# One more pair of up-projection tiles by half-size products, with the last gate's first half summed during the out-projection

## The chip, the cores and the metric

The kernel runs on one core of a Trainium2 chip. Times are microseconds (us) of device time, the median of several runs; beside it stands one profiled execution, whose trace gives the time of each instruction.

The engines are named as in the profile: PE is TensorE (PEld its weight loads), DVE is VectorE, ACT is ScalarE, POOL is GpSimd, SP is SyncE, which here only issues transfers. ACT and POOL issue some transfers too.

## The reference

One decoder layer on 512 tokens of width 1024, all in float32. Sub-layer 1 is a normalised, modulated input projection, two groups of heads (a gated recurrence of 4 heads, and sparse attention), and an output projection. Sub-layer 2, which the change touches most, is a gated MLP of width 2816 with a causal depthwise convolution over 3 tokens:

```python
mod = cs @ w_ada[l] + b_ada[l]
sh1, sc1, gt1, sh2, sc2, gt2 = [m[:, None, :] for m in jnp.split(mod, 6, axis=-1)]
...
x = x + gt1 * mix
h2 = rmsnorm(x, norm2_g[l]) * (1.0 + sc2) + sh2
u = causal_dwconv(h2 @ w_up[l], conv_w[l], conv_b[l])
a, v = jnp.split(u, 2, axis=-1)
x = x + gt2 * ((jax.nn.silu(a) * v) @ w_down[l])
```

Here `cs` is silu of the conditioning vector `c`. The last gate, `gt2`, is a row of 1024 numbers, the product of `cs` with 1024 columns of `w_ada`.

## The kernel before

**Numbers.** A float32 matrix is split into a high and a low part (`split`: ScalarE copies to the rounded type, VectorE subtracts), and a product is three matmuls: high by high, high by low, low by high (`mm3`, lines 156 to 158). Some low parts are formed without VectorE: ScalarE writes the negated rounded value, and a transfer from GpSimd's queue adds the source to it (`added`, lines 260 and 1695).

**Out-projection** (L1577 on). The outputs of the recurrence are normalised per row tile of 128 tokens (`hg_mix`: matmuls, square on ScalarE, sum on VectorE, the reciprocal square root `rstd`, which is one VectorE operation and one on GpSimd, then the scaling `on`), transposed (`hg_flip`) and split. Then eight blocks of the product (`out_mm`, four row tiles by two halves) are added to the residual `x1` (`out_sum`). The loop of L1948 does the second halves; for each row tile it sums squares (`out_norm`: again a root on GpSimd), scales to `hx`, transposes (`h2_flip`) and modulates and splits for the MLP.

**Up-projection.** There are 22 tiles of 128 hidden columns, each with two halves (`a` and `v`), so 44 steps numbered `st`; two tiles make a pair `j`, of four steps. A step in plain form is 8 blocks of the inner dimension by `mm3`: 24 matmuls on 512 tokens. A unit (pairs `NB` = 2 to `NU` = 8, so seven of them) computes the even tile of its pair as a 2 x 2 block product (halves of the inner dimension by halves of the tokens) in seven products instead of eight, at 4 x 3 matmuls on 256 tokens each: 84 half-width matmuls; the odd tile stays plain, 48 full-width matmuls. The first two pairs are plain (the prologue), and so are the last two (steps 36 to 43).

**What sets the order.** Every engine works through its instructions in the order of the program; that order is written out by hand, in strings of tokens: `PRO` for the prologue, `UNIT` for each unit (a prime means: of the next pair), `PLAIN` for the last steps (a leading A: the next weight's low part by an accumulating transfer; the digit: how many steps of the gate). `P1` to `P7` are products, `p` is the convolution, `n`, `s`, `f` form sums and splits of weights, `x` takes one entry from a list of splits of finished values, `g` advances the gate. So an instruction that waits holds up what stands behind it on its engine.

**The gate** (`ada_last`). `gt2` is built in two halves of 512 columns. Each is eight transfers of 128 x 512 weights and eight multiply-adds on VectorE, then a split and two matmuls with a matrix of ones, and a copy back. All transfers are in SyncE's queue. The first half goes through one buffer (the second half of `gt2` itself), one transfer and multiply-add per `g`: three in the prologue and one in each unit. The second half goes through buffers of the general pool during the plain steps.

**Memory.** Most long-lived blocks lie in 33 granules of 4 KB per partition. The finished values of the MLP are kept as `gP`, `gQ` and others for the down-projection, which is a half-size scheme again, in three phases. Where granules are short, `gQ` of the pairs in `AWAY` is written to memory (`park`, from ScalarE's queue) and read back during the first phase (`load_away`); its products stand in the second phase.

Of the kernel before, what the change touches and what calls it, by code (L numbers as in the profile page):

```python
# [20 lines left out]
P = 128  # L21
# [19 lines left out]
NB = 2  # L41
NU = 8
AWAY = (0, 1)
CUT = {"B": 6, "C": 7}
ADD = (1, 1)
PLAIN = "2 A1 1 1 A2 1 1 1"
PRO = ("t t g x M1 M2 t t t t F3 M3 F4 t A5 q0 M4 q1 q2 F6 q3 M5 M6 A7 x q4 g x q5 x t x n1' ns' f2' nc' n5' q6 na' g s4' m0' x x M7 m1' x f6' f7' x x x x f4'")
UNIT = ("P1 S P5 w n1' ns' x f3 B0 P6 P2 B1 V x f2' nc' n5' h1 x p-1 f4' P7 x m0' P3 h0' W p2 g p0 na' C0 P4 x x x C1 s4' p1 x m1' x f6' x x x f7'")
# [63 lines left out]
def hybrid_layer_kernel(ctx: ExitStack, tc: tile.TileContext, d: dict, out: bass.AP, dbg=None):  # L112
# [1164 lines left out]

    def hg_mix(i):
        ps = PS("hgo")
        for h in range(4):  # L1280
            AD, QP, S = As[h // 2]
            j = h % 2
            pe.matmul(ps[:, h * P:(h + 1) * P], AD[:, j, i], HV[j][:, i, h // 2 * P:h // 2 * P + P], start=True,
                      stop=(i == 0))
            if i:
                pe.matmul(ps[:, h * P:(h + 1) * P], QP[:, j, i * P:(i + 1) * P], S[:, j, i - 1], start=False, stop=True)
        sq = TMP([P, 512], tag="sqh")
        sc.activation(sq, ps, AF.Square)
        s = SM([P, 8], "hss")
        ve.tensor_reduce(s[:, 0:4], sq.rearrange("p (h e) -> p h e", h=4), AX.X, ALU.add)  # L1290
        r = SM([P, 8], "hrs")
        rstd(r[:, 0:4], s[:, 0:4], 1.0 / P, 4.0 * EPS)
        on = TMP([P, 4, P], tag="on")
        ve.tensor_tensor(on, ps.rearrange("p (h e) -> p h e", h=4),
                         r[:, 0:4].unsqueeze(2).to_broadcast([P, 4, P]), ALU.mult)
        ons[i] = on

    def hg_flip(i):
        on = ons.pop(i)
# [5 lines left out]
        for pr in range(2):  # L1305
            ve.scalar_tensor_tensor(t[:, 2 * pr:2 * pr + 2], ps[:, pr * 256:pr * 256 + 256]
                                    .rearrange("p (h t) -> p h t", h=2), hgg,
                                    HGT[pr][:, :, i * P:(i + 1) * P], ALU.mult, ALU.mult)
        split(m[:, 0], m[:, 1], t)
        mixH[i] = m  # L1310
# [88 lines left out]
    def ada_last(s, res):  # L1399
        for q in range(2):  # L1400
            acc = res[:, q * 512:(q + 1) * 512]
            c0 = s * D + q * 512
            gp.memset(acc, 0.0)
            sp.dma_start(acc[0:1], d["b_ada"][:, c0:c0 + 512])
            for k in range(KT if q else 0):
                raw = TMP([P, 512], tag="ada2r")
                sp.dma_start(raw, ada_view[:, k, c0:c0 + 512])
                if k:
                    yield
                    ve.scalar_tensor_tensor(acc, last, cs[:, k - 1:k], acc, ALU.mult, ALU.add)  # L1410
                last = raw
            for k in range(0 if q else KT):
                last = res[:, 512:]
                if k:
                    ve.scalar_tensor_tensor(acc, last, cs[:, k - 1:k], acc, ALU.mult, ALU.add)
                sp.dma_start(last, ada_view[:, k, c0:c0 + 512])
                if k < KT - 1:
                    yield
            yield
            ve.scalar_tensor_tensor(acc, last, cs[:, k:k + 1], acc, ALU.mult, ALU.add)  # L1420
            hi = TMP([P, 512], F32R, tag="rhi")
            lo = TMP([P, 512], F32R, tag="rlo")
            split(hi, lo, acc)
            yield
            ps = PS()
            pe.matmul(ps, onesr, hi, start=True, stop=False)
            pe.matmul(ps, onesr, lo, start=False, stop=True)
            sc.copy(acc, ps)
            yield


# [145 lines left out]
    for i in range(NT):  # L1577
        x1.append(G([D], s="x1"))
        sp.dma_start(x1[i], x_view[:, i])
    next(gate1)  # L1580
    hg_mix(0)
    next(gate1)
    hg_mix(1)
    out_mm(0, 0, KN)
    cols_sum(acol)
    hg_flip(0)
    hg_mix(2)
    hg_mix(3)
    out_mm(1, 0, KN)
# [4 lines left out]
    hg_flip(1)  # L1594
    hg_flip(2)
    out_mm(3, 0, KN)
# [148 lines left out]
    def do_(j, tok):  # L1745
# [30 lines left out]
        elif tok == "x":  # L1776
            step(1)
        elif tok == "g":
            next(ada2, None)
        elif tok == "t":  # L1780
# [64 lines left out]
    def park(j, st22, st34):  # L1845
        if j in AWAY:
            sc.dma_start(pk26[:, AWAY.index(j)], f32(gQ.pop(j)))
        sc.dma_start(pk22[:, j], f32(st22))
        sc.dma_start(pk34[:, j], f32(st34))
# [93 lines left out]

    gt2 = wp.tile([P, D], F32, tag="xin", name="gt2", bufs=1)
    ada2 = ada_last(5, gt2)
    lo_half, hi_half, full = slice(0, 256), slice(256, 512), slice(0, 512)
    nst = 2 * NFF
    for i in range(NT):  # L1948
# [6 lines left out]
        out_sum(i, 1)  # L1955
        sc.dma_start(x1d[:, i], x1[i])
        out_norm(i)
        if i:
            h2_scale(i - 1, 0)
            h2_scale(i - 1, 1)  # L1960
# [12 lines left out]
    for tok in PRO.split():  # L1973
# [7 lines left out]
        elif tok[0] == "q":  # L1981
            up_post(int(tok[1]))
        elif tok[0] in "txg":
            do_(1, tok)
        else:
            do(NB - 1, tok)
# [6 lines left out]
    for st in range(first, nst):  # L1993
# [7 lines left out]
        for _ in range(int(PLAIN.split()[st - first][-1])):  # L2001
            next(ada2, None)

    look()
    up_post(nst - 2, False)
# [102 lines left out]
```

## Time and profile before

| | |
|---|---|
| median of 3 runs | 674.73 us (674.6 to 674.8) |
| the profiled execution | 674.35 us, its span 672.6 us |
| granted TensorE clock | 1.0 |
| busy share of the span | PE 99%, PEld 84%, DVE 86%, ACT 58%, POOL 9% |
| out-projection, first matmul to last | 273.7 to 326 us |
| up-projection | 326.9 to 563.8 us (first unit's products from 372.3) |
| down-projection | from 564.2 us |

A row of the timeline reads: start in us, duration in us, engine, line, operation, out<-in, shape, count; in brackets the time that the engine stood idle just before, and what ended that. Matmuls are pipelined, so a matmul's duration is longer than the distance to the next one; the distance between starts is what counts. In a row of windows, each engine has its busy time and its number of instructions in that stretch.

### The profile page before, as it was taken

The numbers are of one execution on the slowest core, as the hardware profiler recorded it, in microseconds if no ns is written. First come the engines' busy times: TensorE is split into PE (matmuls) and PEld (weight loads), VectorE is DVE, ScalarE is ACT, GpSimd is POOL, SyncE is SP. The second block draws the span as 40 slices with busy tenths as digits, with TensorE's granted clock in tenths as the row PEclk, the third lists the DMA queues.
The fourth block names the chain that finished last, engine by engine and source line by source line (L and its number), as shares of the span: only waits on it lengthen the run. The fifth ranks groups of instructions, "written<-read, shape, count | busy, mean of one in ns | idle before, by whom it ended". The sixth has DMA issues, their size and how long they took to land.

```text
span 672.6 us, 10869 instructions
## 1 busy us (share of the span) xinstructions
PE 664.9 (99%) x3999; PEld 565.1 (84%) x3999; DVE 577.8 (86%) x1155; ACT 392.6 (58%) x757; POOL 60.0 (9%) x80
## 2 busy tenths in 40 slices
PE   8999999999999999999999999999999999999998
PEld 4678898788898889888998888989888888888886
DVE  5688988999998997687878988998898789988787
ACT  5564446666677688335665766667675455553431
POOL 1006144200000000200000011010110000000000
PEclk9999999999999999999999999999999999999999
DMA  9998444388042132435436677986779773979932
GB/s 279 287 322 269 145 157 138 106 288 254 11 147 95 33 107 99 172 96 161 140 95 172 179 196 198 242 218 175 187 181 277 217 234 124 393 259 398 388 112 94
DMA packets 110473, 128.52 MB, mean 191 GB/s; under 512 B 7067, under 2 KB 84691, under 8 KB 110421
## 3 DMA queue, kind: packets, MB, share of 16 engines
q1 hardware_dynamic: 103541, 106.89, 51.1%
q0 software_dynamic: 2448, 8.91, 6.9%
q10 hardware_dynamic: 4432, 12.04, 4.7%
q8 instruction: 31, 0.51, 0.3%
q14 instruction: 21, 0.17, 0.1%
HBM read 105.01 MB, written 13.90 MB: 177 GB/s over the span
## 4 chain that ended last, share of the span: by engine, by line
PE 92%; SPq 3%; DMA 2%; DVE 1%; issue 0%; ACTq 0%; ACT 0%
PE u L156 11%; PE u L158 11%; PE u L157 11%; PE dn L157 5%; PE dn L156 5%; PE dn L158 5%; PE pT L156 3%; PE pT L158 3%; PE pT L157 3%; PE F L1059 3%; PE oT L1087 3%; PE oh L158 2%; PE oh L156 2%; PE oh L157 2%; SPq L317 2%; PE lev L1188 2%
## 5 line engine op out<-in xcount | busy, mean ns | idle before, releaser
L156 PE MATMUL u<-h2h,whi 128*128 128x512 f32 (+1 forms) x208 | 78.0, 375 | 0.0
L157 PE MATMUL u<-h2l,whi 128*128 128x512 f32 (+1 forms) x208 | 77.8, 374 | 0.0
L158 PE MATMUL u<-h2h,wlo 128*128 128x512 f32 (+1 forms) x208 | 77.6, 373 | 0.0
L153 DVE TENSOR_TENSOR wlo<-raw,whi 128x1024 fp32r<-128x1024 f32 (+1 forms) x38 | 44.5, 1170 | 6.7 <-ACT whi L152 6.5
L152 ACT CAST whi<-raw 128x1024 fp32r<-128x1024 f32 (+1 forms) x38 | 38.3, 1008 | 18.8 <-PE u L157 7.3
L158 PEld LDWEIGHTS u<-h2h,wlo 128*128 128x128 f32 x208 | 39.2, 188 | 7.5 <-DVE wlo L153 0.4
L156 PEld LDWEIGHTS u<-h2h,whi 128*128 128x128 f32 x208 | 39.3, 189 | 6.0
L157 PEld LDWEIGHTS u<-h2l,whi 128*128 128x128 f32 x208 | 39.3, 189 | 5.8
L1027 ACT ACTIVATE pt<-pt,mx 128x128 f32<-128x128 f32 (+3 forms) x64 | 35.9, 562 | 11.8 <-DVE mx L1011 10.7
L1634 DVE SCALAR_TENSOR_TENSOR y<-u,cv,y 128x511 f32<-128x511 f32 x44 | 32.8, 745 | 11.4 <-ACT y L1633 11.4
L156 PE MATMUL pT<-hT,whi 128*128 128x512 f32 x96 | 39.2, 408 | 0.0
L1638 ACT ACTIVATE y<-y 128x512 f32<-128x512 f32 x21 | 13.3, 633 | 42.0 <-DVE y L1635 42.0
L158 PE MATMUL pT<-hT,wlo 128*128 128x512 f32 x96 | 37.7, 393 | 0.0
L157 PE MATMUL pT<-hT,whi 128*128 128x512 f32 x96 | 37.6, 391 | 0.0
L1011 DVE CUSTOM_DVE_ANT_0 pt<-S,cmask 128x128 f32<-128x128 f32 (+3 forms) x64 | 29.7, 484 | 6.5 <-PE S L1006 6.3
L1066 ACT COPY pT<-F 128x512 f32<-128x512 f32 (+2 forms) x52 | 25.9, 503 | 14.4 <-PE F L1059 11.2
L1635 DVE SCALAR_TENSOR_TENSOR y<-u,cv,y 128x510 f32<-128x510 f32 x44 | 32.9, 749 | 1.6
L1633 ACT ACTIVATE y<-u,cv 128x512 f32<-128x512 f32 x44 | 33.8, 771 | 0.0
L393 POOL TENSOR_TENSOR hrs<-hrs,mhalf 128x4 f32<-128x4 f32 (+2 forms) x16 | 20.0, 1259 | 136.4 <-DVE hrs L392 136.3
L157 PE MATMUL u<-h2l,w 128*128 128x256 f32 (+1 forms) x84 | 28.0, 333 | 0.0
L156 PE MATMUL u<-h2h,w 128*128 128x256 f32 (+1 forms) x84 | 28.0, 333 | 0.0
L158 PE MATMUL u<-h2h,w 128*128 128x256 f32 (+1 forms) x84 | 28.0, 333 | 0.0
(456 smaller groups left out, 2079.2 us busy)
## 6 DMA issues: line engine op xcount, KB each, us to landing
raw<-in_w_up SPq DMA_DIRECT2D x44, 512.0 KB, 5.6
aw<-in_w_ada SPq DMA_DIRECT2D x24, 512.0 KB, 3.6
raw<-in_w_down SPq DMA_DIRECT2D x10, 1024.0 KB
ada<-in_w_ada SPq DMA_DIRECT2D x32, 256.0 KB, 5.8
wlo<-raw POOLq DMA_DIRECT2D x15, 512.0 KB, 4.6
raw<-in_w_in SPq DMA_DIRECT2D x7, 1024.0 KB, 6.1
rawd<-in_w_down SPq DMA_DIRECT2D x12, 512.0 KB, 10.3
pk<-st ACTq DMA_DIRECT2D x11, 512.0 KB, 4.0
```

What stands on the lines that cost most here:

```text
L152: sc.copy(hi, src)
L153: (eng or ve).tensor_tensor(lo, src, f32(hi), ALU.subtract)
L156: pe.matmul(o, ah, bh, start=start, stop=False, skip_group_check=True)
L157: pe.matmul(o, ah, bl, start=False, stop=False, skip_group_check=True)
L158: pe.matmul(o, al, bh, start=False, stop=stop, skip_group_check=True)
L1011: ve.tensor_tensor_reduce(pt[:, sl], ps[:, sl], cmask[:, 512 - W:512], -1.0, 1e30, ALU.add, ALU.min, mx[:, e:e + 1])
L1027: sc.activation(pt[:, sl], pt[:, sl], AF.Exp, bias=mx[:, e:e + 1], scale=-1.0, accum_out=su[:, h % 2, e:e + 1])
L1059: pe.transpose(ps[:, j * P:(j + 1) * P], src[:, j * P:(j + 1) * P], ident)
L1066: sc.copy(pT, ps[:, 0:n * P])
L1633: sc.activation(y, u, AF.Identity, bias=cv[:, 132 + c:133 + c], scale=cv[:, 88 + c:89 + c])
L1634: ve.scalar_tensor_tensor(y[:, 1:], u[:, :T - 1], cv[:, 44 + c:45 + c], y[:, 1:], ALU.mult, ALU.add)
L1635: ve.scalar_tensor_tensor(y[:, 2:], u[:, :T - 2], cv[:, c:c + 1], y[:, 2:], ALU.mult, ALU.add)
```

## The change

- `NU` is 9: one more pair (steps 36 to 39) becomes a unit, and four plain steps are left.
- `AWAY` has pairs 0 to 3 instead of 0 and 1, and `park` stores them from GpSimd's queue.
- `ada_last` is made ready ahead of the out-projection, and split into finer steps: multiply-add, transfer, copy to the high part, subtraction, matmuls, copy back. Its first half has its transfers in GpSimd's queue and is advanced inside the out-projection: between the root and the scaling of `hg_mix` 1 and 3, between copy and subtraction of `hg_flip` 2, and ahead of and behind `out_norm` of each row tile. Its end (last multiply-add, split, matmuls, copy) stands in the prologue (`G`, one step each). The second half has its transfers in SyncE's queue into a part of the constants' tile and is advanced by `g` (two steps) in the units.

```diff
-NU = 8
-AWAY = (0, 1)
+NU = 9
+AWAY = (0, 1, 2, 3)
-PLAIN = "2 A1 1 1 A2 1 1 1"
-PRO = ("t t g x M1 M2 t t t t F3 M3 F4 t A5 q0 M4 q1 q2 F6 q3 M5 M6 A7 x q4 g x q5 x t x n1' ns' f2' nc' n5' q6 na' g s4' m0' x x M7 m1' x f6' f7' x x x x f4'")
+PLAIN = "1 A0 0 A0"
+PRO = ("t t x M1 M2 t t t t F3 M3 F4 t A5 G q0 G M4 q1 q2 F6 q3 M5 G M6 A7 x q4 x q5 G x t x n1' ns' f2' nc' n5' q6 na' s4' m0' x x M7 m1' g x f6' f7' x x x x f4'")
...
     def ada_last(s, res):
         for q in range(2):
             acc = res[:, q * 512:(q + 1) * 512]
+            last = cb[:, C_LMASK:C_LMASK + 512] if q else res[:, 512:]
             c0 = s * D + q * 512
             gp.memset(acc, 0.0)
-            sp.dma_start(acc[0:1], d["b_ada"][:, c0:c0 + 512])
-            for k in range(KT if q else 0):
-                raw = TMP([P, 512], tag="ada2r")
-                sp.dma_start(raw, ada_view[:, k, c0:c0 + 512])
-                if k:
-                    yield
-                    ve.scalar_tensor_tensor(acc, last, cs[:, k - 1:k], acc, ALU.mult, ALU.add)
-                last = raw
-            for k in range(0 if q else KT):
-                last = res[:, 512:]
+            gp.dma_start(acc[0:1], d["b_ada"][:, c0:c0 + 512])
+            for k in range(KT):
                 if k:
                     ve.scalar_tensor_tensor(acc, last, cs[:, k - 1:k], acc, ALU.mult, ALU.add)
-                sp.dma_start(last, ada_view[:, k, c0:c0 + 512])
-                if k < KT - 1:
-                    yield
-            yield
+                yield
+                (sp if q else gp).dma_start(last, ada_view[:, k, c0:c0 + 512])
+                yield
             ve.scalar_tensor_tensor(acc, last, cs[:, k:k + 1], acc, ALU.mult, ALU.add)
             hi = TMP([P, 512], F32R, tag="rhi")
             lo = TMP([P, 512], F32R, tag="rlo")
-            split(hi, lo, acc)
+            sc.copy(hi, acc)
+            yield
+            ve.tensor_tensor(lo, acc, f32(hi), ALU.subtract)
             yield
             ps = PS()
             pe.matmul(ps, onesr, hi, start=True, stop=False)
             pe.matmul(ps, onesr, lo, start=False, stop=True)
+            yield
             sc.copy(acc, ps)
             yield
+
+    def gate_step(n=2):
+        for _ in range(n):
+            next(ada2, None)
...
+    gt2 = wp.tile([P, D], F32, tag="xin", name="gt2", bufs=1)
+    ada2 = ada_last(5, gt2)
+    gate_step()
     next(gate1)
     hg_mix(0)
     next(gate1)
-    hg_mix(1)
+    hg_mix(1, partial(gate_step, 1))
+    gate_step(1)
...
-    hg_mix(3)
+    hg_mix(3, partial(gate_step, 1))
+    gate_step(1)
...
-    hg_flip(2)
+    hg_flip(2, partial(gate_step, 1))
+    gate_step(1)
...
     def park(j, st22, st34):
         if j in AWAY:
-            sc.dma_start(pk26[:, AWAY.index(j)], f32(gQ.pop(j)))
+            gp.dma_start(pk26[:, AWAY.index(j)], f32(gQ.pop(j)))
...
         sc.dma_start(x1d[:, i], x1[i])
+        gate_step(1)
         out_norm(i)
+        gate_step(1)
```

GpSimd's instructions in the out-projection, before (`hrs` and `rs` are the roots of the two normalisations, `hgA` belongs to the recurrence ahead of it, `gt` is `gt2`, `wlo` a low part of an up-projection weight):

```order
L1151 MEMSET hgA_1916 128x1024
L393 TENSOR_TENSOR hrs_3331<-hrs_3331,mhalf 128x4
L393 TENSOR_TENSOR hrs_3353<-hrs_3353,mhalf 128x4
L393 TENSOR_TENSOR hrs_3400<-hrs_3400,mhalf 128x4
L393 TENSOR_TENSOR hrs_3418<-hrs_3418,mhalf 128x4
L393 TENSOR_TENSOR rs_3307<-rs_3307,mhalf 128x1 x4
L1403 MEMSET gt_3611 128x512
L260 DMA wlo_4101<-raw_3690 128x1024
```

And the same place now:

```order
L1407 MEMSET gt_3318 128x512
L1408 DMA gt_3318<-in_b_ada 1x16x32
L1413 DMA gt_3318<-in_w_ada 128x512
L393 TENSOR_TENSOR hrs_3335<-hrs_3335,mhalf 128x4
L393 TENSOR_TENSOR hrs_3357<-hrs_3357,mhalf 128x4
L1413 DMA gt_3318<-in_w_ada 128x512
L393 TENSOR_TENSOR hrs_3406<-hrs_3406,mhalf 128x4
L393 TENSOR_TENSOR hrs_3424<-hrs_3424,mhalf 128x4
L1413 DMA gt_3318<-in_w_ada 128x512 x2
L393 TENSOR_TENSOR rs_3307<-rs_3307,mhalf 128x1
L1413 DMA gt_3318<-in_w_ada 128x512
L393 TENSOR_TENSOR rs_3307<-rs_3307,mhalf 128x1
```

The eight transfers of the gate's first half stand among the roots; the last four follow the four roots of `out_norm` one by one.

VectorE in the last row tile of the out-projection's loop, now (`x` is the residual, `ss` the sum of squares, `hx` the scaled row):

```order
L1511 TENSOR_TENSOR tmp_3858<-oh_3816,gt_90_713 128x512
L1512 TENSOR_TENSOR x_656_3316<-x_656_3316,tmp_3858 128x512
L1411 SCALAR_TENSOR_TENSOR gt_3318<-gt_3318,cs 128x512
L1517 TENSOR_TENSOR ss_3306<-ss_3306 128x1
L392 TENSOR_SCALAR rs_3307<-ss_3306 128x1
L1547 TENSOR_SCALAR hB_3874<-ps_3846,a_711,sh_712 128x128 x4
L1524 TENSOR_SCALAR hx_3879<-x_656_3316,rs_3307 128x512 x2
```

Before, the same rows stood there without the third, the gate's multiply-add.

VectorE at the end of the prologue, before (`raw` is a weight as loaded, `w` and `wlo` low parts of weights, `e` a sum of two quarters of a weight):

```order
L153 TENSOR_TENSOR w_809_4242<-e_4245,w_809_4242 128x512
L1634 SCALAR_TENSOR_TENSOR y_4253<-u_4186,cv,y_4253 128x511
L1635 SCALAR_TENSOR_TENSOR y_4253<-u_4186,cv,y_4253 128x510
L1685 TENSOR_TENSOR raw_4089<-e_4245,raw_4089 128x512
L1415 SCALAR_TENSOR_TENSOR gt_3611<-gt_3611,cs 128x512
L1685 TENSOR_TENSOR raw_4089<-raw_4089 128x512
L153 TENSOR_TENSOR wlo_4266<-raw_4147,whi_4265 128x1024
```

And now:

```order
L153 TENSOR_TENSOR w_812_4263<-e_4266,w_812_4263 128x512
L1642 SCALAR_TENSOR_TENSOR y_4274<-u_4208,cv,y_4274 128x511
L1643 SCALAR_TENSOR_TENSOR y_4274<-u_4208,cv,y_4274 128x510
L1693 TENSOR_TENSOR raw_4103<-e_4266,raw_4103 128x512
L1693 TENSOR_TENSOR raw_4103<-raw_4103 128x512
L153 TENSOR_TENSOR wlo_4285<-raw_4166,whi_4284 128x1024
```

The gate's multiply-add between the two subtractions on the weight is gone from this place.

More of the change, by code (lines that the diff above doesn't have):

```diff
@@ L1276, in hybrid_layer_kernel, with hg_mix @@
     mixH = [None] * NT
-    def hg_mix(i):
+    def hg_mix(i, between=lambda: None):
         ps = PS("hgo")
@@ L1292, in hg_mix @@
         rstd(r[:, 0:4], s[:, 0:4], 1.0 / P, 4.0 * EPS)
+        between()
         on = TMP([P, 4, P], tag="on")
@@ L1296, in hg_mix, with hg_flip @@
         ons[i] = on
-    def hg_flip(i):
+    def hg_flip(i, between=lambda: None):
         on = ons.pop(i)
@@ L1308, in hg_flip @@
                                     HGT[pr][:, :, i * P:(i + 1) * P], ALU.mult, ALU.mult)
-        split(m[:, 0], m[:, 1], t)
+        sc.copy(m[:, 0], t)
+        between()
+        ve.tensor_tensor(m[:, 1], t, f32(m[:, 0]), ALU.subtract)
         mixH[i] = m
@@ L1777, in do_ @@
             step(1)
-        elif tok == "g":
-            next(ada2, None)
+        elif tok in ("g", "G"):
+            gate_step(2 if tok == "g" else 1)
         elif tok == "t":
@@ L1942, in dn_out @@
         sp.dma_start(out_view[:, i, cols], t)
-    gt2 = wp.tile([P, D], F32, tag="xin", name="gt2", bufs=1)
-    ada2 = ada_last(5, gt2)
     lo_half, hi_half, full = slice(0, 256), slice(256, 512), slice(0, 512)
@@ L1982, in hybrid_layer_kernel @@
             up_post(int(tok[1]))
-        elif tok[0] in "txg":
+        elif tok[0] in "txgG":
             do_(1, tok)
@@ L2001, in hybrid_layer_kernel @@
         for _ in range(int(PLAIN.split()[st - first][-1])):
-            next(ada2, None)
+            gate_step()
+    assert next(ada2, 0) == 0
     look()
```

## The prediction

> **What bounds the kernel now.** I read the page first (busy shares, then the chain of waits).
>
> ```profile
> span 672.6 us, 10869 instructions
> PE 664.9 (99%) x3999; PEld 565.1 (84%) x3999; DVE 577.8 (86%) x1155; ACT 392.6 (58%) x757; POOL 60.0 (9%) x80
> PE 92%; SPq 3%; DMA 2%; DVE 1%; issue 0%; ACTq 0%; ACT 0%
> ```
>
> TensorE is 92% of the chain that ends last; what other engines hold there lies mostly at the start, before its work begins. But a busy share of 99% is modelled, so I checked starts: second view, the stages; third, the timeline of TensorE.
>
> ```profile
> core 0: us, PE busy (x) PEld busy (x) DVE busy (x) ACT busy (x) POOL busy (x), PEclk, DMA share, GB/s
> 395.00:416.00 21.00, 21.00 (x134) 19.05 (x133) 18.63 (x34) 13.74 (x25) 1.73 (x2) 1.00 0.85 225
> 526.00:562.00 36.00, 36.00 (x161) 29.80 (x160) 29.20 (x44) 17.80 (x28) 1.75 (x2) 1.00 0.67 213
> ```
>
> The first stretch is one unit (a pair of tiles by half-size products and its two neighbours), the second lies in the plain tiles.
>
> ```profile
> 395.04 0.28 PE L156 MATMUL ux<-hS,w 128*128 128x256 f32 x1
> 395.16 0.28 PE L157 MATMUL ux<-hS,w 128*128 128x256 f32 x1
> ...
> 500.18 0.28 PE L156 MATMUL ux<-hS,w 128*128 128x256 f32 x1
> ...
> 526.13 0.39 PE L158 MATMUL u<-h2h,wlo 128*128 128x512 f32 x1
> ...
> 561.94 0.39 PE L157 MATMUL u<-h2l,whi 128*128 128x512 f32 x1
> ```
>
> From the first product into "ux" of one unit to that of five units later: 105.14 us, so 21.03 us a unit. Half-width matmuls start 0.12 us apart. In the plain stretch, 161 matmuls touch the window; two had begun before it, so 159 start between 526.13 and 561.94: 35.81/158 = 0.2266 us apart. A unit is 84 half-width and 48 full-width matmuls: 84 x 0.12 + 48 x 0.2266 = 20.96, and 21.03 was measured. So TensorE stands still for hardly 0.07 us a unit, and not at all in the plain tiles. The granted clock is 1.00 in both. Whoever wants to gain here must take matmul columns away, or one of the few real waits; whoever delays another engine pays only beyond that engine's slack.
>
> **The extra pair.** Four plain stages (two tiles, both halves of the MLP) become a unit. Before: 4 x 24 matmuls x 0.2266 = 21.75 us. After: 21.03. That takes away 0.72 us, once. The saving is one eighth of the columns of two tiles (3072 of 24576), shrunk because a half-width matmul costs 0.120 where half of a full one is 0.113: 84 x 0.0067 = 0.56 us is lost that way.
>
> The Trainium skill (TensorE: Matmul & The Clock Gate, "Wait — 56ns, not 53.3ns?") puts warm starts at N/2.4 GHz plus about 2.5 ns. That would be 0.2158 and 0.1092 us, and a saving of 48 x 0.2158 - 84 x 0.1092 = 1.18 us, an estimate from that page. The trace differs at both widths (0.2266, 0.120), so the sum goes by 0.72.
>
> Can VectorE feed one more unit? It is busy 18.63 of 21 us in one, and five in a row cost no time; the plain stretch needs less (29.20 of 36). The second half of the gate (one multiply-add and one transfer a unit) takes exactly the place that the first half had, so units stay as they were. Cost 0. If the unit did starve, one more multiply-add a unit (0.745 us, row below) is the scale.
>
> **A wait that goes.** Just ahead of the first unit the trace has one of the few waits of TensorE in this stage.
>
> ```profile
> 373.28 0.75 DVE L1415 SCALAR_TENSOR_TENSOR gt<-gt,cs 128x512 f32<-128x512 f32 x1
> 373.94 0.69 DVE L1685 TENSOR_TENSOR raw<-raw 128x512 f32<-128x512 f32 x1
> 374.55 1.22 DVE L153 TENSOR_TENSOR wlo<-raw,whi 128x1024 fp32r<-128x1024 f32 x1
> ...
> 375.42 0.40 PE L157 MATMUL u<-h2l,whi 128*128 128x512 f32 x1
> 375.82 0.50 PE L158 MATMUL u<-h2h,wlo 128*128 128x512 f32 x1
> 376.15 0.40 PE L156 MATMUL u<-h2h,whi 128*128 128x512 f32 x1
> ...
> 375.82 0.19 PEld L158 LDWEIGHTS u<-h2h,wlo 128*128 128x128 f32 x1 [0.43 <-DVE wlo L153]
> ```
>
> The low part of a weight is formed too late; two starts are 0.40 and 0.33 us apart instead of 0.227: 0.28 us lost. The gate's multiply-add at 373.28 stands right ahead of that form; in the changed order of VectorE nothing of the gate stands there (two of its multiply-adds leave the prologue, a multiply-add and a subtraction come in earlier). The form then ends some 0.66 us sooner, more than the 0.43 that it was late. Bounds 0 and 0.28; I take 0.28, since VectorE has a hole of 2.70 us between the added operations and this place:
>
> ```profile
> 352.23 0.75 DVE L1634 SCALAR_TENSOR_TENSOR y<-u,cv,y 128x511 f32<-128x511 f32 x1 [2.70 <-ACT y L1633]
> ```
>
> **The gate's first half in the out-projection.** Seven multiply-adds and eight loads come in, and the loads stand in GpSimd's queue, among the reciprocal square roots. The multiply-adds are put into holes:
>
> ```profile
> 275.18 0.69 DVE L1294 TENSOR_TENSOR on<-hgo,hrs 128x512 f32<-128x512 f32 x1 [1.13 <-POOL hrs L393]
> ...
> 291.76 0.69 DVE L153 TENSOR_TENSOR mixH<-og,mixH 128x512 fp32r<-128x512 f32 x1 [0.69 <-ACT mixH L152]
> ...
> 311.51 0.89 DVE L1522 TENSOR_SCALAR hx<-x,rs 128x512 f32<-128x512 f32 x2 [0.66 <-POOL rs L393]
> ...
> 314.30 0.69 DVE L1510 TENSOR_TENSOR x<-x,tmp 128x512 f32<-128x512 f32 x1
> 315.78 0.16 DVE L1515 TENSOR_TENSOR ss<-ss 128x1 f32<-128x1 f32 x1 [0.79 <-ACT sq L1512]
> ...
> 321.30 0.69 DVE L1510 TENSOR_TENSOR x<-x,tmp 128x512 f32<-128x512 f32 x1
> ...
> 331.33 0.87 DVE L1522 TENSOR_SCALAR hx<-x,rs 128x512 f32<-128x512 f32 x2
> ```
>
> Each takes 0.745 us, about 0.66 until the next one starts (373.28 to 373.94 in the chain of rows above). The holes are 1.13, 0.69 and 0.79 us. On time they cost nothing. What is late if one is not? Behind it stand the sum of squares, the root on GpSimd, the scaled rows "hx", then the transposes on TensorE, and that slack is thin:
>
> ```profile
> 332.60 0.46 PEld L1532 LDWEIGHTS ps<-cb,hx 128*128 128x128 f32 x4
> ```
>
> "hx" of the last row tile ends at 331.33 + 0.87 = 332.20: 0.40 us ahead of its transposes. So the price is the delay of VectorE above 0.40 us, and one delay carries through all later row tiles, whose chains have no other hole. What can be late is the load. A load is issued after the root of one row tile and wanted before the sum of the next.
>
> ```profile
> 310.93 0.55 POOL L393 TENSOR_TENSOR rs<-rs,mhalf 128x1 f32<-128x1 f32 x1 [24.84 <-DVE rs L392]
> 316.20 0.56 POOL L393 TENSOR_TENSOR rs<-rs,mhalf 128x1 f32<-128x1 f32 x1 [4.72 <-DVE rs L392]
> ...
> L1415 DVE SCALAR_TENSOR_TENSOR gt<-gt,cs x7: 742/745/746, 362.7 to 474.4; 128x512 f32<-128x512 f32 x7
> ...
> gt<-in_w_ada SPq DMA_DIRECT2D x8, 256.0 KB, 2.8
> ...
> L1695 POOL DMA_DIRECT2D wlo<-raw x13: 862/872/890, 376.0 to 502.5; - x13
> ...
> DMA to landing us min/median/max: 4.5/4.6/8.3
> ...
> 331.55 0.35 SPq L1416 DMA_DIRECT2D gt<-in_w_ada  x1
> ```
>
> No load of this size from GpSimd is in the trace. The same 256 KB from SyncE land after 2.8 us, of which 0.35 is issue; GpSimd's issue takes 0.872: 2.8 + 0.52 = 3.3 us, my value. Above it stand GpSimd's own transfers, of twice the size: 4.6 us median, 8.3 at most. The tightest is the fifth load: issued at 310.93 + 0.55 = 311.48, wanted at 314.30 + 0.60 = 314.90. At 3.3 us it lands at 314.8: no delay. At 4.6 us it lands at 316.1, the sum starts 0.66 later at 316.74 instead of 315.78, 0.96 late: TensorE loses 0.96 - 0.40 = 0.56. So 0 to 0.56; I take 0.1, near the like-sized row. The sixth has 5.1 us (316.76 to 321.90).
>
> The other half of the two-step split (copy, then subtraction one step later) adds no instruction: those of the first half leave the last unit for the prologue, with two matmuls either way. Cost 0, between -0.1 and 0.3 if the prologue's ScalarE chain shifts.
>
> **Parking.** Two more granules are stored and read back, and all four stores leave ScalarE's queue for GpSimd's.
>
> ```profile
> 399.84 0.33 ACTq L1847 DMA_DIRECT2D pk<-gQ  x1
> ...
> 397.01 0.87 POOL L1695 DMA_DIRECT2D wlo<-raw  x1 [8.21 <-ACT gP L152]
> 409.36 0.86 POOL L1695 DMA_DIRECT2D wlo<-raw  x1 [11.49 <-ACT wlo L1694]
> ...
> 580.18 0.42 SPq L1899 DMA_DIRECT2D gQ<-pk  x1
> ...
> L156 PEld LDWEIGHTS dn<-whi,gQ x28: 187/188/188, 593.9 to 623.1; 128*128 128x128 f32 x28
> ```
>
> GpSimd waits 8.21 and 11.49 us ahead of its accumulating transfers; a store of 0.87 us of issue fits in between, and behind it waits only the next such transfer. The reloads: the second one was issued at 580.18, its product is wanted from 593.9; two more of 0.5 MB each, wanted one product pair (24 x 0.2266 = 5.4 us) later, have as much room. Cost 0; without that cover 0.9 us for a late accumulate.
>
> **Sum.** -0.72 - 0.28 + 0.1 = -0.9 us on the profiled execution of 674.35 us (span 672.6, 1.75 around it): 673.45. The median of the three runs, 674.73, lies 0.38 above that execution: **673.8 us**, or 0.13% less. A measurement of this kernel can tell about 0.2% from no change, 1.35 us: 673.38 and 676.08 are the bounds.
>
> **Rivals.**
> (1) *The gate's loads come late* (the slower side). Place: the fifth load, ahead of the second row tile's sum. From a landing of 5.0 us on (delay 1.36, TensorE loses 0.96) it eats the gain; from 6.4 us on the kernel is slower by over 0.2%; at 8.3 us the delay is 4.66, the loss 4.26: 674.73 - 1.0 + 4.26 = 678.0. For it: VectorE takes its work in order, and the stage has 0.40 us of slack. Against it: the transfers of 2.8 us, and 8.3 is the maximum of 13. There is a mechanism for it: the two "hx" operations (0.87 us) start exactly where the loads are issued, 311.51 against 311.48. If they hold the issue up, 3.3 becomes 4.2 (673.9 us) and 4.6 becomes 5.5 (a loss of 1.4: 675.2).
> The Trainium skill (SBUF — State Buffer, "Who interferes with whom") says that VectorE's two-port modes, which such scalar operations can enter, shut GpSimd out from writing the descriptors of its own transfers. No run here shows it yet.
> (2) *Only the pair counts*: the first unit still waits, or the prologue's added operations make a wait of that size: 674.73 - 0.72 + 0.1 = 674.1; with the 0.56 of the out-projection 674.6.
> (3) *Faster than the rows allow*: half-width matmuls of the new pair at half a full one's 0.113. It would save 0.72 + 0.56 + 0.28 = 1.56: 673.2. Against it: every unit so far.
> By the spacing of the Trainium skill (the page on TensorE above) the pair would save 1.18, with the wait 1.46: 673.3 us, the same rival; the rows above speak against it.
> (4) *Parking disturbs* a unit or the down-projection: 0.9 us for each late accumulate or reload, at most four: 677.4. Slots and queues have room, so little.
>
> **How the numbers follow.** Forecast (673.4 to 674.3): 0.58. Rival 2 (674.1 to 674.8): 0.20. Rival 1: 0.12, about half of it over 676.08. Rival 3: 0.06. Rival 4: 0.04. Faster by over 0.2%: 0.08 (rival 3 and the lower edge of the forecast). Slower: 0.09 (most of rival 1 and 4). Within: 0.83. The range 673.2 to 675.4 leaves out the long landings of rival 1, rival 4 and the edge of rival 3.
>
> **What would show it.** Right: units of 21.03 us, eight of them; no 0.43 us wait of the weight load ahead of the first; "hx" and its transposes where they were; landings of the gate's loads from GpSimd near 3.3 us. Wrong: a wait of VectorE for a load ahead of a sum of squares, transposes waiting for "hx", or a weight load waiting for an accumulate behind a store.

## The result: 4.4 us slower

| | before | changed |
|---|---|---|
| median (6 runs each) | 674.7 us (674.3 to 675.2) | 679.09 us (678.64 to 679.85) |
| span of the profiled execution | 672.6 us | 678.1 us |
| granted TensorE clock | 1.0 | 1.0 |

The ratio is 1.0065, 95% interval 1.0052 to 1.0078. The forecast was 673.8 us, and no change that can be measured. The page of the changed kernel begins:

```profile
span 678.1 us, 10964 instructions
PE 667.3 (98%) x4035; PEld 566.2 (84%) x4035; DVE 581.0 (86%) x1165; ACT 396.3 (58%) x765; POOL 70.1 (10%) x95
...
PE 71%; DVE 12%; DMA 6%; ACT 4%; SPq 3%; issue 2%; ACTq 0%; DVEq 0%
```

TensorE's part of the chain that ended last falls from 92% to 71%: VectorE, ScalarE and transfers now set the end over a long stretch. To find it I added up TensorE's starts by stage, in us (each row is the first start of a stage to that of the next):

| | before | changed |
|---|---|---|
| out-projection | 53.13 | 53.15 |
| up-projection until the first unit's "ux" | 46.88 | 47.34 (the gate's two matmuls) |
| units: seven, now eight | 147.45 | 174.08 |
| plain tiles behind them | 43.01 | 20.79 (four stages and the gate's two matmuls less) |
| down-projection until the last matmul | 104.87 | 104.89 |

Only the units differ from the forecast. Eight of 21.03 us would be 168.2; they took 5.86 more. Together the five stages are 4.9 us longer than before. The two spans differ by 5.5: 0.45 of the rest lies ahead of the out-projection, which the kernels whose warm-up is unchanged started anywhere between 273.1 and 274.2 us, and 0.14 behind the last matmul. In the timeline of TensorE, the first product into "ux" of each unit:

```profile
374.67 0.28 PE L156 MATMUL ux<-hS,w 128*128 128x256 f32 x1
396.59 0.28 PE L156 MATMUL ux<-hS,w 128*128 128x256 f32 x1
417.62 0.28 PE L156 MATMUL ux<-hS,w 128*128 128x256 f32 x1
440.19 0.28 PE L156 MATMUL ux<-hS,w 128*128 128x256 f32 x1
463.19 0.28 PE L156 MATMUL ux<-hS,w 128*128 128x256 f32 x1
485.67 0.28 PE L156 MATMUL ux<-hS,w 128*128 128x256 f32 x1
506.70 0.28 PE L156 MATMUL ux<-hS,w 128*128 128x256 f32 x1
```

The units are 21.92, 21.03, 22.57, 22.99, 22.49, 21.03 ... us long. The view of waits between 370 and 560 us says what the weight loads waited for (total, times, longest):

```profile
PEld u L156 <- ACT u L1775: 3.2, 3, 1.1
PEld u L158 <- DMA wlo<-raw: 2.2, 3, 1.0
PEld u L158 <- DVE wlo L153: 1.0, 1, 1.0
```

Three different releasers, but one cause behind two of them. In every unit ScalarE begins a low part (L1702; called the **form** below) from a weight that SyncE loads. Its timeline, units 2 to 4:

```profile
411.83 1.06 ACT L1702 ACTIVATE wlo<-raw 128x1024 fp32r<-128x1024 f32 x1 [4.56 <-DMA raw<-in_w_up]
434.82 1.06 ACT L1702 ACTIVATE wlo<-raw 128x1024 fp32r<-128x1024 f32 x1 [4.48 <-DMA raw<-in_w_up]
457.29 1.06 ACT L1702 ACTIVATE wlo<-raw 128x1024 fp32r<-128x1024 f32 x1 [3.97 <-DMA raw<-in_w_up]
```

And SyncE's issues of the loads that these three wait for:

```profile
405.10 0.37 SPq L223 DMA_DIRECT2D raw<-in_w_up  x1
...
428.17 0.37 SPq L223 DMA_DIRECT2D raw<-in_w_up  x1
...
451.16 0.37 SPq L223 DMA_DIRECT2D raw<-in_w_up  x1
```

This is a **loop**. From the start of the form to the next unit's issue (the buffer comes free when VectorE is through) pass 428.17 - 411.83 = 16.34 us, and 451.16 - 434.82 = 16.34 again: ScalarE and VectorE work through their order. From issue to form, the **lead**, pass 6.73, 6.65 and 6.13 us. So the loop takes 23.07, 22.99 and 22.5 us, and those are the lengths of units 3 to 5 (22.57, 22.99 and 22.49), but for 0.5 us of slack that unit 3 still had. TensorE's own 21.03 us can be kept only while the lead is at most 4.69 us. Before, the same place in the second unit read so in ScalarE's timeline, with the load issued at 403.25:

```profile
407.95 1.06 ACT L1694 ACTIVATE wlo<-raw 128x1024 fp32r<-128x1024 f32 x1 [1.97 <-PE u L158]
```

There ScalarE waited for TensorE, not for the load, which was ready within 4.70 us; in the units after it, where ScalarE did wait for the load, the leads were 4.3 to 4.65 us. What else moves at that time are the stores of the parked granules, now from GpSimd's queue in units 1 to 4. The transfers between 370 and 560 us, changed kernel (issuer, count, size, median us to landing):

```profile
pk<-gQ POOLq DMA_DIRECT2D x4, 512.0 KB, 6.1
```

and before:

```profile
pk<-gQ ACTq DMA_DIRECT2D x2, 512.0 KB, 3.0
```

(The 3.0 us is one landing: the trace tells that of one of the two stores only.)

The third wait, on VectorE, is the one that the forecast saw going away; counted from "ux" it lies inside the first unit. It grew: TensorE's starts there are 376.39, 377.31 and 377.65, 1.26 us for two matmuls of 0.227: 0.8 us lost, where it had been 0.28.

```profile
376.39 0.39 PE L157 MATMUL u<-h2l,whi 128*128 128x512 f32 x1
377.31 0.50 PE L158 MATMUL u<-h2h,wlo 128*128 128x512 f32 x1 [0.53 <-DVE wlo L153]
377.65 0.40 PE L156 MATMUL u<-h2h,whi 128*128 128x512 f32 x1
```

Followed backwards, VectorE and ScalarE release each other through the prologue without a hole, up to this place in ScalarE's timeline of the changed kernel:

```profile
346.73 1.03 ACT L261 CAST whi<-raw 128x1024 fp32r<-128x1024 f32 x1
348.23 0.62 ACT L1418 CAST rhi<-gt 128x512 fp32r<-128x512 f32 x1 [0.47 <-DVE gt L1415]
348.76 0.77 ACT L1641 ACTIVATE y<-u,cv 128x512 f32<-128x512 f32 x1
```

Before, "y" followed "whi" by 0.94 us (346.26 to 347.20); now by 2.03, because the gate's cast, and its wait for the gate's multiply-add, stand between. All of VectorE's and ScalarE's work enters the units 1.09 us later, counted from the start of the up-projection. TensorE reaches them 0.46 us later, because of the gate's two matmuls, so the low part is some 0.6 us later for it than before, and the wait of 0.28 us became 0.8.

### The profile page after: what moved, and what is told of

Read it like the earlier page. It is cut to its first block, busy times and chain, and to the rows that moved or that the text cites. A ratio compares the mean times of both kernels' runs of the same rounds, so it can differ in the third digit from the quotient of the medians.

```text
span 678.1 us, 10964 instructions
## 1 busy us (share of the span) xinstructions
PE 667.3 (98%) x4035; PEld 566.2 (84%) x4035; DVE 581.0 (86%) x1165; ACT 396.3 (58%) x765; POOL 70.1 (10%) x95
## 4 chain that ended last, share of the span: by engine, by line
PE 71%; DVE 12%; DMA 6%; ACT 4%; SPq 3%; issue 2%; ACTq 0%; DVEq 0%
PE dn L156 5%; PE dn L158 5%; PE dn L157 5%; PE u L156 5%; PE u L158 5%; PE u L157 5%; DMA raw<-in_w_up 4%; PE pT L156 3%; PE pT L158 3%; PE pT L157 3%; PE F L1059 3%; PE oT L1087 3%; PE oh L158 2%; PE oh L156 2%; PE oh L157 2%; DVE y L1643 2%
## 5 line engine op out<-in xcount | busy, mean ns | idle before, releaser
L158 PE MATMUL u<-h2h,wlo 128*128 128x512 f32 (+1 forms) x200 | 74.9, 374 | 1.5 <-DMA wlo<-raw 0.8
L156 PE MATMUL u<-h2h,whi 128*128 128x512 f32 (+1 forms) x200 | 75.0, 375 | 0.0
L157 PE MATMUL u<-h2l,whi 128*128 128x512 f32 (+1 forms) x200 | 74.8, 374 | 0.0
L153 DVE TENSOR_TENSOR wlo<-raw,whi 128x1024 fp32r<-128x1024 f32 (+1 forms) x35 | 40.8, 1166 | 7.4 <-ACT whi L152 7.2
L158 PEld LDWEIGHTS u<-h2h,wlo 128*128 128x128 f32 x200 | 37.7, 188 | 9.8 <-DMA wlo<-raw 2.2
L152 ACT CAST whi<-raw 128x1024 fp32r<-128x1024 f32 (+1 forms) x35 | 35.1, 1004 | 16.0 <-PE kva L158 4.4
L156 PEld LDWEIGHTS u<-h2h,whi 128*128 128x128 f32 x200 | 37.8, 189 | 5.4
L156 PE MATMUL u<-hS,wq 128*128 128x256 f32 x96 | 27.3, 285 | 1.9 <-ACT u L1775 1.9
L1702 ACT ACTIVATE wlo<-raw 128x1024 fp32r<-128x1024 f32 x15 | 15.9, 1061 | 22.1 <-DMA raw<-in_w_up 22.1
L152 ACT CAST wq<-raw 128x512 fp32r<-128x512 f32 x40 | 24.6, 617 | 7.2 <-DVE st L153 5.9
```

Of the source, the lines that this page charges most:

```text
L152: sc.copy(hi, src)
L153: (eng or ve).tensor_tensor(lo, src, f32(hi), ALU.subtract)
L156: pe.matmul(o, ah, bh, start=start, stop=False, skip_group_check=True)
L157: pe.matmul(o, ah, bl, start=False, stop=False, skip_group_check=True)
L158: pe.matmul(o, al, bh, start=False, stop=stop, skip_group_check=True)
```

## Experiments: which part of the change

In the comparisons below the kernel before stood at 674.66 to 674.82 us. "Excess" is the units' length over 8 x 21.03 us, from the trace. Three theories were tested: **queue** (GpSimd's queue makes a store late), **count** (four stores are too many), **lag** (the 1.09 us).

**Stores from ScalarE's queue again**

```diff
-            gp.dma_start(pk26[:, AWAY.index(j)], f32(gQ.pop(j)))
+            sc.dma_start(pk26[:, AWAY.index(j)], f32(gQ.pop(j)))
```

> Edit: the four parking stores of a unit's granules are issued by ScalarE again, everything else of the change kept. Three theories of the 5.5 us that the units lost. Queue (POOL's queue makes a store late and long: it landed 5.8 to 6.4 us after its issue in the changed kernel, 3.0 us from ScalarE before, so that it is still moving when the unit's next weight load starts, and that load lands in 6.7 us instead of about 4.7): the store's landing falls back to about 3 us, the load of each unit to at most 4.7 us, the starts of the units stand 21.03 us apart again from the second on, and of the 5.5 us only the first unit's wait of some 0.6 us stays: 674.2 to 675.0. Count (four stores of 512 KB instead of two are too many bytes, whichever queue): the third and fourth unit keep about 23 us, 676.5 to 679. Lag (VectorE and ScalarE enter the units 1.1 us later behind TensorE since the gate's split stands in the prologue's chain): no change, 678.5 to 679.5.

677.28 us, ratio 1.0037 (1.0025 to 1.0050); excess 3.02. The leads are 5.4, 5.3 and 5.2 us instead of 6.7, 6.6 and 6.1: better by a good microsecond, but not 4.7. The queue is a part of it, not all.

**The gate's split in idle time**

```diff
-PRO = ("... t A5 G q0 G M4 q1 q2 F6 q3 M5 ...")
+PRO = ("... t A5 q0 G M4 q1 q2 G F6 q3 M5 ...")
...
             ve.scalar_tensor_tensor(acc, last, cs[:, k:k + 1], acc, ALU.mult, ALU.add)
+            if not q:
+                yield
             hi = TMP([P, 512], F32R, tag="rhi")
...
         ve.scalar_tensor_tensor(y[:, 2:], u[:, :T - 2], cv[:, c:c + 1], y[:, 2:], ALU.mult, ALU.add)
         ys[st] = y
+        mid()
...
-            up_post(int(tok[1]))
+            up_post(int(tok[1]), mid=partial(gate_step, int(tok == "q2")))
```

> Edit: the last multiply-add of the gate's first half stands behind the first tile's, and its cast behind the third tile's first ScalarE operation, each in idle time of its engine, instead of both ahead of the first tile's; the stores stay on POOL's queue. Queue: the first unit's wait (0.69 us in the changed kernel) goes, and VectorE enters the units 1.1 us earlier, which is used up once by the late loads: 1.1 us of the 5.5 at most come back, 677.8 to 678.6, units 3 to 5 still over 22 us. Count: the same numbers as queue. Lag: with the 1.1 us back no unit waits, 673.5 to 674.2.

677.68 us, ratio 1.0047 (1.0035 to 1.0060); excess 4.40. The wait in the first unit is gone (that unit takes 21.03 us), and 1.5 us come back: a little more than the 1.1 at most of queue and count, far from the 5.5 of lag. So lag is a part of it, and not all.

**Both**

> Edit: both of the first two edits, so ScalarE's stores and the gate's split in idle time. Queue: no wait of TensorE left in the units, starts 21.03 us apart, and the prediction's sum for the extra pair and the first unit's wait comes out: 673.4 to 674.2, below the kernel before. Count: units 3 and 4 stay long, 675.5 to 678. Lag: 673.5 to 674.2 as queue, so this run tells only count from the others.

675.84 us, ratio 1.0019 (1.0010 to 1.0028); excess 1.72, nearly all in units 4 and 5. Queue alone is refuted; count held so far. Its view of waits:

```profile
PEld u L156 <- ACT u L1778: 1.6, 2, 0.9
PEld u L156 <- DVE u L1782: 0.4, 2, 0.2
```

**The kernel before, its two stores from GpSimd's queue** (the first edit the other way round)

> Edit: the kernel before with one line changed: its two parking stores are issued by POOL's queue instead of ScalarE's. Queue: two units of about 23 us instead of 21.03, less the 2 us by which ScalarE was ahead of TensorE's release in the second unit: 675.5 to 678.0. Count and lag: nothing moves, 674.4 to 675.0, or a little less, since ScalarE no longer stands 1.97 us behind the stores in a unit.

675.58 us, ratio 1.0012 (1.0003 to 1.0021). But in its trace no unit is longer than before by more than 0.06 us, and the leads beside GpSimd's stores are 4.80 and 4.86 us, though the stores took 5.4 to 5.6 us to land. So the same store, from the same queue, held a load for 4.8 us here and for 6.7 us in the changed kernel. What made its median 0.9 us slower its trace does not show; the profiled execution, 674.78 us, was one of its fast ones.

## Experiments: what made the same store dear

Two things differed between those stores: the step between a partition's rows in memory (8 KB with two parked granules in a row, 16 KB with four), and the load of the gate's second half, which is issued among the unit's weight loads.

**Each parked granule in a tensor of its own**, in the changed kernel

```diff
-    pk26 = hbm.tile([P, len(AWAY), 2, 2, 256], F32, name="pk26")
+    pk26 = [hbm.tile([P, 2, 2, 256], F32, name=f"pk26_{n}") for n in range(len(AWAY))]
...
-            gp.dma_start(pk26[:, AWAY.index(j)], f32(gQ.pop(j)))
+            gp.dma_start(pk26[AWAY.index(j)], f32(gQ.pop(j)))
```

> Edit: the changed kernel, with the four parked granules in four tensors of their own in HBM instead of one whose row holds all four: a partition's 4 KB then follow the next one's, where they stood 16 KB apart (8 KB apart in the kernel before, with two). Stores stay on POOL's queue. So far a unit's first weight load was ready 4.5 us after its issue without a store beside it, 4.8 to 4.9 us beside POOL's store in the kernel before with 8 KB, 6.1 to 6.7 us beside it in the changed kernel with 16 KB. Stride (the 16 KB steps make the store slow for those behind it): 4.9 us or less in all four units; what stays is the first unit's wait and little else, 674.5 to 675.8. Gate load (the load of the gate's second half, issued among the unit's weight loads, holds them): 6.1 to 6.7 us as before the edit, 678.5 to 679.5. Count (four stores in a row): no difference from 679.1.

678.7 us (1.0046 to 1.0070), leads 6.8, 6.2 and 6.6 us. The step in memory is not it.

**The same in the kernel with both first edits**

> Edit: the kernel with ScalarE's stores and the gate's split in idle time (675.84 us, its parked units' first weight load ready after 4.9 to 5.4 us), with the four granules in tensors of their own. Stride: the loads are ready after 4.5 to 4.7 us, no unit over 21.1 us, 673.5 to 674.3, below the kernel before. Gate load and count: no change, 675.4 to 676.2.

676.05 us (1.0012 to 1.0030): no change either.

**Without seven of the gate's loads**

```diff
-                (sp if q else gp).dma_start(last, ada_view[:, k, c0:c0 + 512])
+                if not (q and k):
+                    (sp if q else gp).dma_start(last, ada_view[:, k, c0:c0 + 512])
```

> Edit: the changed kernel without seven of the eight loads of the gate's second half; its multiply-adds run on the first one's values, so the second half of the last gate is another. Gate load: the first weight load of a parked unit is ready within 5 us, 674.5 to 676. Stride and count: the first load's lead does not change by more than 0.3 us (the gate's load is issued behind it), the second pair of weight loads is issued 1.5 to 3 us earlier and the accumulate behind it lands earlier, so that the waits for it go (1.6 us of TensorE's idle) while those for ScalarE's copy stay: 676.8 to 678.5.

679.02 us (1.0053 to 1.0077), leads 6.6, 6.2 and 6.4 us. (This kernel leaves out seven loads, so the second half of its `gt2` is not the reference's; the order of work is the same.) The gate's loads are not it. The view of waits is worth a look:

```profile
PEld u L156 <- ACT u L1776: 4.4, 3, 1.7
PEld u L158 <- DVE wlo L153: 1.0, 1, 1.0
PEld u L158 <- DMA wlo<-raw: 0.3, 1, 0.3
```

The waits for accumulating transfers fell from 2.2 to 0.3 us, and the waits for ScalarE's copy rose from 3.2 to 4.4. The units stayed as long as they were, since the loop sets their length; what TensorE happens to meet first is only where it shows. I had priced those waits one by one, and the time came out 0.5 us above my range.

**Four stores in the kernel before**, from ScalarE

```diff
-AWAY = (0, 1)
+AWAY = (0, 1, 2, 3)
```

> Edit: the kernel before with four granules parked and loaded again instead of two, by ScalarE's queue, in one tensor with 16 KB steps. Stride or count: the loads beside a store are ready after 5.1 to 5.5 us, units 3 and 4 come out at 21.5 to 22 us as in the kernel with both first edits, 675.2 to 676.6. Gate load: 674.4 to 675.0, and what the two extra reloads of 512 KB cost in the down-projection.

676.1 us (1.0011 to 1.0028). The leads in its first four units are 4.27, 4.52, 5.36 and 5.30 us. In units 2 and 3 the same stores stand at the same distance ahead of the load (3.4 us) and yet differ by 0.84. I compared the transfers from 0.5 us ahead of the load's issue to 2.5 us behind it. Unit 2 (kind of queue: packets, MB, share of the 16 transfer engines):

```profile
q10 hardware_dynamic: 212, 0.63, 59.5%
q1 hardware_dynamic: 613, 0.31, 36.5%
```

Unit 3:

```profile
q10 hardware_dynamic: 212, 0.63, 59.6%
q1 hardware_dynamic: 551, 0.28, 33.0%
q8 instruction: 1, 0.02, 2.7%
```

There is one packet more, of the instruction queue, and the loads moved 62 packets fewer. The page of the changed kernel counts them:

```profile
q8 instruction: 32, 0.52, 0.3%
```

Each is 16 KB and took 0.9 to 1.5 us. 32 of them go with 4,035 matmuls and as many weight loads, one for 252 instructions of TensorE; a unit has 264. So a packet comes once a unit, nearly at the same place in each, and that place is set by how many instructions TensorE's program has ahead of it. The Trainium skill (Runtime: NRT & Kernel Launch, "Instruction fetch mechanics") states the same size, 16 KiB or 256 instructions, brought by a queue of the engine's own while it runs. It calls the cost of crossing such a boundary "mostly hidden", which is a cost to the engine that fetches; the table below shows one to the transfers beside it.

I then sorted the 95 such loads of all fourteen traces (all units but each trace's last) by two things: who stores, and whether such a packet starts between 2 us ahead of the load's issue and 3.1 us behind it. Median lead, range, and number of units:

| | no packet near | packet near |
|---|---|---|
| no parking store | 4.06 us (3.94 to 4.22), 9 | 4.48 us (4.14 to 5.01), 34 |
| store from ScalarE | 4.46 us (4.06 to 4.96), 16 | 5.28 us (5.05 to 5.94), 14 |
| store from GpSimd | 4.98 us (4.80 to 5.45), 10 | 6.49 us (6.13 to 6.76), 12 |

Within each of the lower two rows, the two columns do not overlap. (The table includes the four runs below; they fill most of the first column. In three units the form waited for TensorE and not for the load, so that their leads are upper bounds.) The bounds of "near" were drawn to fit the first ten traces: the upper one lies between a packet 3.01 us behind the issue (lead 6.76, GpSimd's store) and one 3.19 us behind it (lead 4.27, ScalarE's). What tests them are the runs below. In the kernel before the packet came 4.7 and 4.0 us behind the load's issue in the two units with stores, and only then slid in. With GpSimd's stores in that kernel it came 5.6 and 5.4 us behind, which goes with the leads of 4.8 us there. The other instruction queue, q14 (21 packets of 8 KB in the changed kernel), does not go with the leads: none of its packets starts from 3 us ahead of the loads of units 2 and 4 until they are through, and those leads were 6.73 and 6.13 us.

## Experiments: moving the packet

At the start of the program stand 24 matmuls that are meant to warm TensorE up. Cutting them into pieces adds instructions ahead of everything else and nothing to compute.

```diff
-    for _ in range(WARM):
-        pe.matmul(warm, wrm[:, 0:P], wrm, start=True, stop=True)
+    for n in range(4 * WARM):
+        pe.matmul(warm[:, n % 4 * 128:][:, :128], wrm[:, 0:P], wrm[:, :128], start=True, stop=True)
```

and the same for the other two groups of eight.

**144 more instructions, ScalarE's stores, split in idle time**

> Edit: the kernel with ScalarE's stores and the gate's split in idle time (675.84 us); its 24 warming matmuls of 512 columns at the very start are each cut in four of 128, so that TensorE's program has 144 more instructions ahead of everything else. Reason: the instruction queue moves a packet of 16 KB, 0.9 to 1.3 us long, about every 253 TensorE instructions, so once a unit of 265. In all runs so far a parked unit's first weight load was ready after 4.3 to 4.9 us (ScalarE's store) or 4.8 to 5.5 us (POOL's) where that packet came over 3.9 us behind the load's issue, and after 5.1 to 5.9 or 6.1 to 6.7 us where it came between 1.9 us ahead of the issue and 3 us behind it. Fetch (the packet is the cause): 144 instructions move it 11 us earlier in every unit, out of the way; loads ready within 4.3 to 4.9 us, all units 21.03 us, 673.4 to 674.3. Count (four stores in a row, the packet a coincidence): units 3 and 4 stay at 21.7 to 22 us, 675.4 to 676.3.

674.0 us, ratio 0.9993 (0.9984 to 1.0001), from 675.84; leads 4.1 to 4.9; all eight units 21.03 us; excess 0.00. Four stores in a row are still there, so count is refuted too.

**144 more instructions in the changed kernel, nothing else**

> Edit: the changed kernel, with the same 144 more TensorE instructions at the start and nothing else. Fetch: the first loads of the parked units are ready after 4.8 to 5.5 us instead of 6.1 to 6.7, which gives back 1.2 us in each of units 2 to 4; the first unit's wait of 0.7 us and about 1 us of the rest stay: 675.0 to 676.6. Count: 678.5 to 679.5.

675.06 us, ratio 1.0006 (0.9997 to 1.0015), **4.0 us less than the changed kernel**; excess 0.99 instead of 5.86, nearly all of it the wait in the first unit. ScalarE's timeline, the same three units as above:

```profile
410.27 1.06 ACT L1702 ACTIVATE wlo<-raw 128x1024 fp32r<-128x1024 f32 x1 [2.70 <-DMA raw<-in_w_up]
431.66 1.06 ACT L1702 ACTIVATE wlo<-raw 128x1024 fp32r<-128x1024 f32 x1 [2.87 <-DMA raw<-in_w_up]
452.91 1.07 ACT L1702 ACTIVATE wlo<-raw 128x1024 fp32r<-128x1024 f32 x1 [2.75 <-DMA raw<-in_w_up]
```

and SyncE's issue of the load for the second of these rows, the third unit's:

```profile
426.62 0.37 SPq L223 DMA_DIRECT2D raw<-in_w_up  x1
```

So that lead is 5.04 us. The transfers from 2 us ahead of the third unit's load to 3.1 us behind it, first in the changed kernel:

```profile
q10 hardware_dynamic: 288, 0.79, 41.1%
q0 software_dynamic: 166, 0.55, 37.1%
q1 hardware_dynamic: 563, 0.29, 19.9%
q8 instruction: 1, 0.02, 1.1%
```

then in this one:

```profile
q10 hardware_dynamic: 288, 0.79, 40.4%
q0 software_dynamic: 166, 0.55, 39.8%
q1 hardware_dynamic: 568, 0.29, 21.1%
```

Stores (q10 from ScalarE, q0 from GpSimd) and loads (q1) are the same to the packet or nearly so; the lead is 6.65 us with the instruction packet and 5.04 without.

**256 more instructions, in the kernel with both first edits** (the first two groups in pieces of 64 columns, the third in three of 168): the packets are back at their old places, one later in the program

> Edit: as the first kernel of this call, but the warming matmuls cut into more pieces, 256 more TensorE instructions, so that the packets fall where they fell in the kernel with 675.84 us, one packet later in the program. Fetch: 675.3 to 676.3, the loads of units 2 to 4 ready after 5.0 to 5.9 us. If cutting the warming matmuls does something of its own, this one is as fast as the first of this call.

675.69 us, ratio 1.0016 (1.0007 to 1.0025); leads 5.4, 5.3 and 5.1, excess 1.91. It is the place of the packet that counts, not the cutting.

**144 more instructions, cut otherwise**, in the same kernel

```diff
+    for n in range(8 * WARM):
+        pe.matmul(warm[:, n % 8 * 64:][:, :64], wrm[:, 0:P], wrm[:, :64], start=True, stop=True)
...
+    for n in range(3 * WARM2):
+        pe.matmul(warm[:, n % 3 * 168:][:, :168], wrm[:, 0:P], wrm[:, :168], start=True, stop=True)
```

> Edit: the kernel with ScalarE's stores, the gate's split in idle time and 144 more TensorE instructions at the start (674.0 us), with those instructions made otherwise: the first eight warming matmuls are cut in pieces of 64 columns and the next eight in pieces of 168, the last eight are left whole. Reason: with all cut in 128 columns TensorE was busy 2.1 of the 4 us from 12 us on and the granted clock fell to 0.50 from 16 to 18 us, after which all stood 1.0 us later; with pieces of 64 and 168 columns (256 more instructions) it stayed at 1.00. Fetch: packets out of the way and the 1.0 us back, 672.7 to 673.4, below the kernel before by the prediction's sum and more than its interval. If the clock is not what cost that 1.0 us: 673.7 to 674.3 again.

674.1 us, ratio 0.9992 (0.9983 to 1.0001): no faster than the other way of cutting, so this expectation failed. The fall of the granted clock was real in the profiled execution on which it rested. Windows of the trace of the first kernel with 144 instructions (stretch, length, busy time of PE, PEld, DVE, ACT and POOL, then the granted clock, the DMA share, GB/s):

```profile
12.00:16.00 4.00, 2.10 (x21) 0.67 (x20) 1.08 (x2) 0.48 (x2) 0.12 (x1) 0.85 1.16 303
16.00:20.00 4.00, 3.95 (x19) 3.46 (x21) 2.87 (x8) 2.81 (x9) 0.00 (x0) 0.72 1.06 302
```

and of this kernel's:

```profile
12.00:16.00 4.00, 2.79 (x31) 1.63 (x30) 1.63 (x5) 1.32 (x4) 0.07 (x1) 1.00 1.16 304
16.00:20.00 4.00, 3.96 (x28) 2.25 (x30) 3.60 (x14) 2.88 (x10) 0.00 (x0) 1.00 1.15 316
```

But that execution was the slowest of its kernel's eleven (675.29) and this one the fastest of its eleven (673.40); the medians show no such loss. The two kernels with 144 more instructions and both first edits are the fastest of the study; their 0.69 and 0.65 us below the kernel before are not quite told from no change, since both intervals reach 1.0001.

## Why the prediction was wrong, step by step

- **The bound, the extra pair, the first unit's wait.** Right in size. (The 3072 columns saved are one eighth of the even tile's 24,576, not of both tiles'; the 0.72 does not rest on it.) From the first up-projection product to the down-projection, the last kernel above needs 236.34 us where the one before needed 237.34: -1.00, and the forecast's two terms were -0.72 and -0.28. The changed kernel has -0.72 in it too; 5.6 us of waits more than before lie on top (5.86 less the 0.26 by which the old wait made the first unit longer).
- **The two-step split, "cost 0, between -0.1 and 0.3".** Mis-sized: 1.5 us (5.86 to 4.40). The hole of 2.70 us that I quoted opens behind the first tile's ScalarE operation; the gate's cast stands ahead of it, so it delayed the chain by 1.09 us instead of filling the hole. The term that rested on it, the wait that goes, had the wrong sign in the changed kernel.
- **The gate's loads in the out-projection, +0.1, and rival 1.** The fear was unfounded. The stage took 53.15 us against 53.13. Seven of the loads in the view of that tile (the estimate was 3.3 us to landing, of which 0.872 to issue):

```profile
L1413 POOL DMA_DIRECT2D gt<-in_w_ada x7: 536/588/669, 279.2 to 331.3; - x7
...
DMA to landing us min/median/max: 3.0/3.1/4.7
```

  The last row tile's "hx" still ends 0.40 us ahead of its transposes (331.80 + 0.87 = 332.67, and 333.07). The fifth load, beside "hx", took the longest to issue, 0.67 us, and that harmed nothing.
- **Parking, "cost 0; behind it waits only the next such transfer": the step that failed.** I looked for what waits behind the store in its queue, and nothing does. What is held up stands in another queue: SyncE's weight load, issued 2.6 us after the store. It took 6.1 to 6.7 us beside the stores, where the loop affords 4.69, and units 3 to 5 lost 1.5 to 2.0 us each. The Trainium skill (DMA: Bandwidth & Descriptors, "Issuing engines are not separate DMA queues") says in so many words that transfers of all issuers end on the same 16 engines; that rule spoke against the step, and I did not weigh it. Its other half, that spreading transfers over issuers saves issue time only, does not cover what the table shows: a load beside ScalarE's store took 4.46 us and beside GpSimd's 4.98 without a packet, 5.28 and 6.49 with one, where the issues of the stores differ by 0.2 us.
- **"Can VectorE feed one more unit?"** The wrong question. Busy shares and five quiet units said yes, but the margin was in the loop: 16.34 us of work and at most 4.69 for the load, and before the change the loads took 4.3 to 4.65 of them. That could have been read from the trace of before, and so "cost 0" for one unit more held only while nothing slowed a load.
- **Rival 4** (parking disturbs, at most 677.4) had the right part, with a chance of 0.04, and the wrong price: 0.9 us for a late accumulate, where a parked unit lost up to 2.
- **Reloads** cost nothing, as forecast: the down-projection took 104.89 us after 104.87.

The shares of the 5.86 us do not add, since each part alone decides how much of the slack is left for the others: ScalarE's queue for the stores takes 2.8 away (to 3.02), the split's place 1.5 (to 4.40), both 4.1 (to 1.72), the packet's place alone 4.9 (to 0.99), all three everything.

Open stays how one packet holds a load by up to 1.5 us, more than the 0.9 to 1.3 us that those packets took; the traces do not tell the 16 transfer engines apart. Open is also the 0.9 us of the kernel before with GpSimd's stores.

## What to carry to other kernels

A transfer that is "hidden" has to be followed on the transfer engines, not only in its queue: look for the next load that someone waits for, and for the loop of buffer, load and form that it closes. Compare that loop with the bound engine's period before calling a stage unchanged; here 0.04 to 0.4 us of margin were left. And where the program is long and unrolled, as here, look for the instruction packets among the transfers: shifting TensorE's program by 144 instructions told in one run that they mattered.

## What was not expected of the hardware

- Instruction packets of 16 KB, one for 252 TensorE instructions, 0.9 to 1.5 us each in the changed kernel: with one near, a weight load of 512 KB was ready 0.4 us later (medians) without a parking store, 0.8 us later beside a store from ScalarE, 1.5 us later beside one from GpSimd. 144 instructions that compute nothing made a kernel 4.0 us faster.
- The same 512 KB store landed 5.4 to 6.5 us after its issue from GpSimd. From ScalarE only four landings can be read: 3.0 us three times, and 4.7 us once.
- Rows of 4 KB stored 16 KB apart or one behind the other made no difference (679.1 and 678.7 us; 675.84 and 676.05).
